# Hybrid attention and DeltaNet step: queries' rotations dealt out in steps, written engine order in two places more

## The chip, the cores and the metric

One NeuronCore of one Trainium2 chip runs the whole step in one launch. The metric is the device time of a launch in microseconds (us). TensorE is called PE, VectorE DVE, ScalarE ACT, GpSimd POOL and SyncE SP.

## The reference

A two-layer decoder trunk works on 1024 prompt tokens and on 8 decode sequences of 4 new tokens, 1056 columns in all. Layer 0 is latent attention (MLA) with a paged cache, layer 1 a gated DeltaNet; each is followed by a SwiGLU feed-forward. The part that the change touches most is the projection of the queries:

```
a = u @ w_in
c_q = rmsnorm(a[..., :Q_LORA], g_q)
c_kv = rmsnorm(a[..., Q_LORA:Q_LORA + KV_LORA], g_kv)
k_r = rope(a[..., Q_LORA + KV_LORA:], pos)
q = (c_q @ w_uq).reshape(b, t, MLA_HEADS, QK_NOPE + QK_ROPE)
q_rope = rope(q[..., QK_NOPE:], pos)
# rope: concat(x1 * cos - x2 * sin, x2 * cos + x1 * sin)
# every layer: x += post_norm(mixer(pre_norm(x))); x += post_norm(ffn(pre_norm(x)))
```

## The kernel before, in words

Activations lie with features on partitions and the 1056 tokens as columns, which are taken in three groups, `GRP`: 384, 384 and 288. A float32 product is made of three matmuls (`mm3`, L261 to L263): each operand is split into a high part, a copy on ACT (L236), and a low part, a subtraction on DVE (L237). `lin` makes one 128-row output block for one group, in one of eight PSUM banks (`ps`) that the elementwise engines have to empty before PE can use it again.

The norms between sublayers are generators, called jobs: squares are summed (`sqs`, `sqr`), PE adds them over partitions with a product by ones (`norm_sum`, L422), DVE takes an inverse square root in ten small operations (`rsqrt`, L291 to L295), PE spreads it over partitions (`norm_spread`, L440), and DVE scales the activations (L344, L353). Each `lin` calls `tick`, which lets the jobs take a step. Outside `with self.order()` a scheduler sets the order of the instructions on each engine from its own priorities; inside it PE, and each engine named, keeps the order in which the code is written.

The query stage in `mla_latents` runs 12 units of three `lin`s, each with a contraction of 3 × 128 rows (`cqh`, `cql`). The first four (`mla_w_uqr`) give the rotary parts of two heads each: ACT copies them out to `qr`, four DMAs issued by POOL write the half-swapped copy (`araw`, L615), DVE then makes `qr*cos`, `araw*sin` and their sum (L620 to L622, 128x1056), ACT and DVE split the result, and POOL issues two DMAs to DRAM (`qrd`). The other eight (`mla_w_uqn`) are the plain parts of the heads, split straight from PSUM into `qh` and `ql` and sent to DRAM (`qd`). The rotary key (`raw[5]`, an `araw` tile as well) is turned after the second plain unit. `absorb` multiplies the decode queries by `w_uk`. The attention that follows loads its queries from `qd` and `qrd` (L1025).

`dn_out` is the output product of the DeltaNet (`out_proj`, L1167), whose norms overlap the beginning of the second feed-forward, `ffn(1)`. `Decode` reads cache pages (`pg`, L1795) beside the output product of layer 0; its two accumulators lie in a pool of that stage.

Of the kernel before, what the change touches and what calls it, by code (L numbers as in the profile page):

```python
# [8 lines left out]
F32 = mybir.dt.float32  # L9
# [6 lines left out]
P = 128  # L16
# [11 lines left out]
LAT = (1, 2)  # L28
NPART = 3
# [6 lines left out]
TICKS = (1, 0), (1, 2), (1, 4), (2, 0), (2, 2), (2, 4)  # L36
# [70 lines left out]
class K:  # L107


    def __init__(self, ctx, tc, I, O):  # L110
# [6 lines left out]
        self.gap = GAP[0]  # L117
# [211 lines left out]
    def boundary_group(self, g, acc, h_src, h_dst, post, pre, u, sq, full):  # L329
# [287 lines left out]
    def rotate(self, raw, sw, cos, sin):  # L617

        nc = self.nc
        nc.vector.tensor_tensor(raw, raw, cos, op=ALU.mult)  # L620
        nc.vector.tensor_tensor(sw, sw, sin, op=ALU.mult)
        nc.vector.tensor_tensor(raw, raw, sw, op=ALU.add)  # L622

    def latent_norm(self, raw, part, out, gn, g):
# [3 lines left out]
        for _ in range(LAT[0]):  # L628
            yield 1
        y = self.norm_sum(sq, g, P * len(part))  # L630
        for _ in range(LAT[1]):
            yield 1
# [17 lines left out]
    def first_layer(self, right, top, h1, h2):  # L650
# [4 lines left out]
        with ExitStack() as left:  # L655
# [11 lines left out]
            OL = top.enter_context(self.scope("mlak", "right")).tile([P, 512], F32, name="OL")  # L667
# [12 lines left out]
            with self.banks(**DBANK):  # L680
                with self.order(*EARLY):


                    side = Decode(self, *smp, OL, tab, msk, wk)
# [7 lines left out]
                    pages(1, 1, 0, 1, False)  # L692
                    self.queue = self.store = nc.gpsimd
                    first = [self.raw_weight(I["mla_w_o"][m]) for m in range(3)]
                    self.queue = nc.sync
                    pages(0, 1, 0, 3)
                    pages(1, 1, 1, 3, False)
                    pages(0, 1, 3, 4)
                    pages(0, 0, 0, 1)
                    pages(1, 1, 3, 4, False)  # L700
                    heads(nc.gpsimd, (0, 0), (0, 1), (1, 0), (1, 1))
                    pages(1, 0, 0, 1, False)
                    pages(0, 0, 1, 4)
                    heads(nc.gpsimd, (2, 0), (2, 1), (3, 0), (3, 1), (4, 0), (4, 1), (5, 0))
# [104 lines left out]
    def mla_project(self, cst):  # L809
# [19 lines left out]
    def mla_latents(self, u, r2, start, ws, araw, gn, wk, cst):  # L829
        nc, I, O, tc, NH = self.nc, self.I, self.O, self.tc, 8  # L830
        with self.banks(ps=8):
# [36 lines left out]


            qs = wk.tile([P, NH * TS_], F32, name="qs")  # L870
            qrs = wk.tile([P, NH * TS_], F32, name="qrs")
            qd = tc.dram_tile([NH, 2, P, TP], F32, name="qd")
            qrd = tc.dram_tile([NH // 2, 2, P, TP], F32, name="qrd")
            qr, sw = {}, {}

            def turned(p):

                self.rotate(qr[p], sw[p], cos, sin)
                for i in range(2):
                    for d in range(2):  # L880
                        nc.gpsimd.tensor_copy(qrs[d * 64:(d + 1) * 64, (2 * p + i) * TS_:(2 * p + i + 1) * TS_],
                                              qr[p][i * 64:(i + 1) * 64, TP:])
                hl = self.S(F32R, "qh"), self.S(F32R, "ql")
                self.split(hl[0][:, :TP], hl[1][:, :TP], qr[p][:, :TP])
                for d in range(2):
                    nc.gpsimd.dma_start(qrd[p, d], hl[d][:, :TP].bitcast(F32))

            def keys():

                sw = araw(0)  # L890
                self.swap(sw, raw[5], nc.gpsimd)
                self.rotate(raw[5], sw, cos, sin)
                h = self.S(F32R, "KRh")
                nc.scalar.activation(h[64:], raw[5][64:], AF.Copy)
                nc.scalar.activation(KR[:64], raw[5][:64], AF.Copy)
                nc.vector.tensor_tensor(KR[64:], raw[5][64:], h[64:].bitcast(F32), op=ALU.subtract)


            pss, absorbed = [], []

            def absorb(hh):
                if not pss:
                    pss.extend(self.psum() for _ in range(2))
                w = absorbed[hh]
                for h4 in range(4):
                    hs = slice((hh * 4 + h4) * TS_, (hh * 4 + h4 + 1) * TS_)
                    for rt in range(2):
                        nc.tensor.matmul(pss[rt][:, hs], w[:, h4 * 256 + rt * P:h4 * 256 + (rt + 1) * P], qs[:, hs],
                                         start=True, stop=True)

            for p in range(NH // 2):
                qr[p], sw[p] = self.S(F32, "qr"), araw(p % 2)
                w = self.weight(I["mla_w_uqr"][p], 384)
                for g in GRP:
                    self.ready(("q", g[0]))
                    ps = self.psum()
                    self.lin(ps, w, cq, 0, g)
                    nc.scalar.activation(qr[p][:, g[0]:g[0] + g[1]], ps[:, :g[1]], AF.Copy)
                self.swap(sw[p], qr[p], nc.gpsimd)
                if p:  # L920
                    turned(p - 1)
            for h in range(NH):
# [12 lines left out]
                if h == 0:  # L935
                    turned(3)
# [1081 lines left out]
```

## Time and profile before

| | |
|---|---|
| three runs | 3140.64, 3153.95, 3154.75 us; median 3153.95 |
| profiled execution | 3136.75 us, its span 3135.1 us |
| mean granted PE clock | 0.982 |
| PE busy | 3022.0 us (96%) |
| DVE busy | 1830.4 us (58%) |
| ACT busy | 1174.2 us (37%) |
| POOL busy | 495.3 us (16%) |

PE is busy nearly throughout, so what can be won is PE's idle time, some 113 us (the span less the busy time), and the time in which its clock was granted at half. A wait is read as "who waited, for what": the engine that stood idle, and the instruction whose end let it go on.

### The profile page before, as it was taken

How to read it: one execution, taken by the hardware profiler on the slowest of the kernel's cores; microseconds unless marked ns; L12 is line 12 of the kernel's file. 1: busy time of each engine (PE TensorE's matmuls, PEld its weight loads, DVE VectorE, ACT ScalarE, POOL GpSimd, SP SyncE). 2: the span in 40 equal slices, each digit the busy share in tenths (PEclk: the TensorE clock that was granted, in tenths of full speed). 3: DMA queues.
4: the chain of work that ended last, by engine and by line, in shares of the span. 5: the costliest groups of instructions: out<-in, count | busy, mean ns of one | idle time of the engine just before them, and what ended most of it. 6: DMA issues, size and time to landing. Idle time of an engine off the chain costs nothing.

```text
span 3135.1 us, 57855 instructions
## 1 busy us (share of the span) xinstructions
PE 3022.0 (96%) x21526; PEld 2800.6 (89%) x21526; DVE 1830.4 (58%) x4234; ACT 1174.2 (37%) x2545; POOL 495.3 (16%) x909
## 2 busy tenths in 40 slices
PE   8799989999999999999999999999989999999998
PEld 8789978888888889999888888888889999999997
DVE  7668757544444444886676667665586444444436
ACT  5345545533333323454444444443542111111121
POOL 1200124344334321121011111111000000000000
PEclk9889999999999999999999999998999999999998
DMA  3564479888788853364322222223231111111113
GB/s 124 165 214 129 134 249 315 291 276 277 241 270 272 270 176 134 122 219 166 124 58 72 79 72 79 74 75 119 82 118 66 41 54 41 44 51 41 48 48 111
DMA packets 286203, 434.52 MB, mean 139 GB/s; under 512 B 60705, under 2 KB 221089, under 8 KB 285922
## 3 DMA queue, kind: packets, MB, share of 16 engines
q1 hardware_dynamic: 220418, 274.51, 27.3%
q0 software_dynamic: 45936, 144.09, 14.2%
q10 hardware_dynamic: 19568, 12.23, 1.3%
q8 instruction: 170, 2.79, 0.4%
q14 instruction: 111, 0.91, 0.1%
HBM read 369.69 MB, written 58.30 MB: 137 GB/s over the span
## 4 chain that ended last, share of the span: by engine, by line
PE 84%; DVE 8%; issue 3%; DMA 3%; ACT 2%; SPq 0%; POOL 0%; ACTq 0%; DVEq 0%; POOLq 0%
PE ps L261 22%; PE ps L262 21%; PE ps L263 21%; PE po L1879 2%; PE sc L1823 2%; PE sc L1100 1%; PE sc L1827 1%; PE tp L1127 1%; PE s L1698 1%; ACT ga L1482 1%; PE s L1695 1%; DVE wl L237 1%; PE ps L422 1%; PE s L1686 1%; PE ga L1605 1%
## 5 line engine op out<-in xcount | busy, mean ns | idle before, releaser
L261 PE MATMUL ps<-oh,wh 128*128 128x384 f32 (+1 forms) x2480 | 816.3, 329 | 6.9 <-ACT wh L236 5.6
L263 PE MATMUL ps<-oh,wl 128*128 128x384 f32 (+1 forms) x2480 | 804.6, 324 | 1.1 <-DVE wl L237 1.1
L262 PE MATMUL ps<-ol,wh 128*128 128x384 f32 (+1 forms) x2480 | 802.6, 324 | 0.0
L236 ACT ACTIVATE wh<-w 128x1024 fp32r<-128x1024 f32 (+3 forms) x300 | 299.2, 1004 | 618.5 <-PE ps L262 523.0
L261 PEld LDWEIGHTS ps<-oh,wh 128*128 128x128 f32 x2480 | 470.0, 190 | 34.1 <-issue 26.0
L263 PEld LDWEIGHTS ps<-oh,wl 128*128 128x128 f32 x2480 | 469.3, 189 | 2.4 <-DVE wl L237 1.9
L262 PEld LDWEIGHTS ps<-ol,wh 128*128 128x128 f32 x2480 | 469.5, 189 | 1.3 <-issue 0.8
L237 DVE TENSOR_TENSOR wl<-w,wh 128x1024 fp32r<-128x1024 f32 (+3 forms) x297 | 342.1, 1159 | 126.8 <-ACT wh L236 124.6
L1795 POOL DMA_DIRECT2D pg<-cache x518 | 283.8, 548 | 460.6 <-PE po L1879 327.3
L261 PE MATMUL ps<-uh,wh 128*128 128x384 f32 (+1 forms) x912 | 310.2, 340 | 8.4 <-ACT wh L236 7.5
L262 PE MATMUL ps<-ul,wh 128*128 128x384 f32 (+1 forms) x912 | 306.1, 336 | 3.0 <-DVE ul L353 3.0
L263 PE MATMUL ps<-uh,wl 128*128 128x384 f32 (+1 forms) x912 | 301.3, 331 | 1.5 <-POOL wl L237 1.5
L261 PE MATMUL ps<-hh,wh 128*128 128x384 f32 (+1 forms) x880 | 294.5, 336 | 0.0
L262 PE MATMUL ps<-hl,wh 128*128 128x384 f32 (+1 forms) x880 | 290.0, 330 | 0.0
L263 PE MATMUL ps<-hh,wl 128*128 128x384 f32 (+1 forms) x880 | 289.3, 329 | 0.0
L261 PEld LDWEIGHTS ps<-uh,wh 128*128 128x128 f32 x912 | 173.6, 190 | 12.2 <-ACT wh L236 7.5
L262 PEld LDWEIGHTS ps<-ul,wh 128*128 128x128 f32 x912 | 173.6, 190 | 5.7 <-DVE ul L353 4.0
L263 PEld LDWEIGHTS ps<-uh,wl 128*128 128x128 f32 x912 | 173.2, 190 | 3.8 <-POOL wl L237 2.0
L261 PEld LDWEIGHTS ps<-hh,wh 128*128 128x128 f32 x880 | 165.3, 188 | 12.1 <-issue 7.9
L262 PEld LDWEIGHTS ps<-hl,wh 128*128 128x128 f32 x880 | 166.2, 189 | 0.9
L263 PEld LDWEIGHTS ps<-hh,wl 128*128 128x128 f32 x880 | 166.0, 189 | 0.1
L568 DVE TENSOR_TENSOR acc<-acc,ps 128x384 f32<-128x384 f32 (+1 forms) x240 | 121.3, 518 | 65.2 <-PE ps L263 63.8
(446 smaller groups left out, 4934.6 us busy)
## 6 DMA issues: line engine op xcount, KB each, us to landing
pg<-cache SPq DMA_DIRECT2D x504, 160.0 KB, 4.0
pg<-cache POOLq DMA_DIRECT2D x510, 128.0 KB, 3.8
w<-ffn_w_in SPq DMA_DIRECT2D x86, 512.0 KB, 4.3
w<-ffn_w_in POOLq DMA_DIRECT2D x52, 512.0 KB, 4.0
w<-ffn_w_out SPq DMA_DIRECT2D x40, 512.0 KB, 4.4
w<-dn_w_in SPq DMA_DIRECT2D x32, 512.0 KB, 3.2
w<-ffn_w_out POOLq DMA_DIRECT2D x26, 512.0 KB, 3.7
qn<-qd SPq DMA_DIRECT2D x64, 128.0 KB, 2.9
```

The lines of the kernel that those rows point to most:

```text
L236: self.nc.scalar.activation(hi, src, AF.Copy)
L237: (lo_eng or self.nc.vector).tensor_tensor(lo, src, hi.bitcast(F32), op=ALU.subtract)
L261: mm(out, ah, bh, start=(i == 0), stop=False)
L262: mm(out, ah, bl, start=False, stop=False)
L263: mm(out, al, bh, start=False, stop=(i == n - 1))
L422: nc.tensor.matmul(ps[:bn, i:i + 1], q[:, b0:b0 + bn], self.ones, start=j == 0, stop=j == len(sq) - 1)
L568: nc.vector.tensor_tensor(acc[m][:, s], acc[m][:, s], po[:, :tn], op=ALU.add)
L1100: mm(o, x["qr"][e][d][:, qsl], KR[:, c], start=False, stop=d == 1)
L1127: self.nc.tensor.transpose(ps[:, j * P:(j + 1) * P], prob[:, kb * P:(kb + 1) * P], self.ident)
L1795: (self.nc.sync, self.nc.gpsimd)[pool].dma_start(self.pages[step, part][c0 + i // 2][:, i % 2], I["cache"][bass.ds(page, 1)].rearrange("o ...
L1823: mm(row(ps, c)[:, :256].rearrange("p (g k) -> p g k", g=2), q(i, c), pgs[c][:, :, i * P:(i + 1) * P], start=i == 0, stop=False)
L1879: nc.tensor.matmul(row(po, c)[:, :256], pT[:, j * P + c * TS_:j * P + (c + 1) * TS_], v, start=j == 0, stop=t < 0 or j == 1)
```

## The change

1. The queries become a function of their own, `mla_queries`, in which PE, ACT and DVE keep the written order. Each rotation is a generator, `away`, and one step of one of them is taken after two of every three `lin`s, from the sixth `lin` on (`WAY`). The key comes first. The product by cos goes from DVE to POOL. Weights are fetched two units ahead. The steps of the latent norms come at ticks (2, 3) in place of (1, 2). `qd` and `qrd` become one DRAM tile for each head and each pair.
2. The three low parts of `mla_w_in` at the start go from POOL to DVE.
3. The two accumulators of `Decode` go to a pool that lives longer, and some issues of pages and head weights change place or queue.
4. In `out_proj` a job waits two more ticks (`LEAD`) before the norm sum of the activations, and `dn_out` with `ffn(1)` keeps PE's written order.
5. The group loop of `dn_start` keeps PE's written order.
6. Each entry of `TICKS`, which sets when the last norm's jobs step in the last chunk of the second feed-forward, is one later.

```diff
-TICKS = (1, 0), (1, 2), (1, 4), (2, 0), (2, 2), (2, 4)
+TICKS = (1, 1), (1, 3), (1, 5), (2, 1), (2, 3), (2, 5)
+LEAD = 2
...
         if post is not None:
+            for _ in range(self.lead):
+                yield 1
             y = self.norm_sum(sq, g, D)
...
-                        ws.append(self.weight(I["mla_w_in"][len(ws)], lo_eng=nc.gpsimd))
+                        ws.append(self.weight(I["mla_w_in"][len(ws)]))
...
+            with self.order(*EARLY[1:3]):
+                return self.mla_queries(raw, cq, ckv, KR, cos, sin, araw, wk, cst)
...
+        def away(x, i, p=None):
+
+            sw = araw(i)
+            self.swap(sw, x, nc.gpsimd)
+            nc.gpsimd.tensor_tensor(x, x, cos, op=ALU.mult)
+            yield 1
+            nc.vector.tensor_tensor(sw, sw, sin, op=ALU.mult)
+            nc.vector.tensor_tensor(x, x, sw, op=ALU.add)
+            yield 1
...
+            hl = [self.S(F32R, "qh")[:, :TP], self.S(F32R, "ql")[:, :TP]]
+            nc.scalar.activation(hl[0], x[:, :TP], AF.Copy)
+            yield 1
+            nc.vector.tensor_tensor(hl[1], x[:, :TP], hl[0].bitcast(F32), op=ALU.subtract)
+            for d in range(2):
+                nc.gpsimd.dma_start(qrd[p][d], hl[d].bitcast(F32))
...
+        go(raw[5], 0)
...
+                if g is GRP[0] and n + 2 < len(units):
+                    ws.append(fetch(units[n + 2]))
+                if lins >= WAY and lins % 3:
+                    step()
+                lins += 1
+            if rotary:
+                go(x, (i + 1) % 3, i)
...
-        self.slack = SLACK[part is not None]
+        self.slack, self.lead = SLACK[part is not None], LEAD
...
-        for g in GRP:
-            self.ready(("u", g[0]))
...
+        with self.order():
+            for g in GRP:
+                self.ready(("u", g[0]))
...
-            with k.weights(*FW[2]):
+            with k.weights(*FW[2]), k.order():
```

On DVE in the query stage, before: rotations of pairs 2 and 3 (`qr`), of which each stands whole in front of the low parts (`ql`) of a plain unit's three PSUM banks; the key (the last row) comes after two plain units.

```order
L237 TENSOR_TENSOR ql_1311<-qr_1151,qh_1310 128x1024
L237 TENSOR_TENSOR ql_1323<-ps_1324,qh_1322 128x384
L237 TENSOR_TENSOR ql_1323<-ps_1336,qh_1322 128x384
L237 TENSOR_TENSOR ql_1323<-ps_1348,qh_1322 128x256
L620 TENSOR_TENSOR qr_1226<-qr_1226,cos_170 128x1056
L621 TENSOR_TENSOR araw_1227<-araw_1227,sin_171 128x1056
L622 TENSOR_TENSOR qr_1226<-qr_1226,araw_1227 128x1056
L237 TENSOR_TENSOR ql_1371<-qr_1226,qh_1370 128x1024
L237 TENSOR_TENSOR ql_1383<-ps_1384,qh_1382 128x384
L237 TENSOR_TENSOR ql_1383<-ps_1396,qh_1382 128x384
L237 TENSOR_TENSOR ql_1383<-ps_1408,qh_1382 128x256
L620 TENSOR_TENSOR araw_595<-araw_595,cos_170 128x1056
```

On DVE at the same place after the change, with the rotations of pairs 2 and 3 again (line numbers are those of the changed kernel; `wl` is the low part of a weight fetched ahead):

```order
L240 TENSOR_TENSOR ql_1437<-ps_1456,qh_1436 128x384
L890 TENSOR_TENSOR araw_1217<-araw_1217,sin_171 128x1056
L891 TENSOR_TENSOR qr_1149<-qr_1149,araw_1217 128x1056
L240 TENSOR_TENSOR ql_1437<-ps_1470,qh_1436 128x256
L240 TENSOR_TENSOR ql_1493<-ps_1494,qh_1492 128x384
L240 TENSOR_TENSOR wl_1509<-w_1506,wh_1508 128x384
L240 TENSOR_TENSOR ql_1493<-ps_1512,qh_1492 128x384
L909 TENSOR_TENSOR ql_1488<-qr_1149,qh_1487 128x1024
L240 TENSOR_TENSOR ql_1493<-ps_1527,qh_1492 128x256
L890 TENSOR_TENSOR araw_1284<-araw_1284,sin_171 128x1056
L891 TENSOR_TENSOR qr_1223<-qr_1223,araw_1284 128x1056
L240 TENSOR_TENSOR ql_1545<-ps_1546,qh_1544 128x384
```

A rotation now stands in two pieces of two and one operations, with one to five emptied banks between them, the cos product is gone from DVE, and the key has come long before.

On POOL, after the change, at the beginning of the queries (L888 is the cos product, L620 the swap's DMAs, `araw_595` the key):

```order
L888 TENSOR_TENSOR araw_595<-araw_595,cos_170 128x1056
L620 DMA araw_1083<-qr_1020 32x1056 x2
L620 DMA araw_1143<-qr_1089 32x1056 x2
L888 TENSOR_TENSOR qr_1020<-qr_1020,cos_170 128x1056
L620 DMA araw_1143<-qr_1089 32x1056 x2
L900 DMA rowsT<-araw_595 64x1056
L620 DMA araw_1217<-qr_1149 32x1056
L888 TENSOR_TENSOR qr_1089<-qr_1089,cos_170 128x1056
```

POOL had only copies and DMA issues there before; now five cos products stand between its DMA issues.

On PE, before, in the beginning of the second feed-forward (`ps<-ones,sqr` is a norm sum over the first group, `ps<-ident,ny` what spreads its root; 29 matmuls stand between the sum and the spread, all but two of them left out here):

```order
L263 MATMUL ps_28475<-oh_27824,wl_27874 128x288
L261 MATMUL ps_28495<-oh_27025,wh_27879 128x288
L422 MATMUL ps_28511<-ones,sqr_28209 128x1 x3
L262 MATMUL ps_28495<-ol_27029,wh_27879 128x288
...
L263 MATMUL ps_28533<-oh_27824,wl_27886 128x288
L440 MATMUL ps_28550<-ident,ny_28513 128x128 x3
L261 MATMUL ps_28559<-oh_27025,wh_27891 128x288
```

On PE, after the change, the same sum and its root's spread:

```order
L266 MATMUL ps_28617<-oh_27710,wl_28597 128x384
L445 MATMUL ps_28687<-ident,ny_28644 128x128 x2
L445 MATMUL ps_28687<-ident,ny_28644 128x32
L427 MATMUL ps_28727<-ones,sqr_28266 128x1 x3
L445 MATMUL ps_28746<-ident,ny_28729 128x128 x3
L264 MATMUL ps_28759<-oh_27014,wh_28604 128x384
```

The spread of the first group's root now stands right behind its sum, with no matmul between them.

## Rows read from the trace of the kernel before

**Rows 1.** Page, part 1: busy time, share of the span and instructions.

```profile
PE 3022.0 (96%) x21526; PEld 2800.6 (89%) x21526; DVE 1830.4 (58%) x4234; ACT 1174.2 (37%) x2545; POOL 495.3 (16%) x909
```

**Rows 2.** What PE waited for, whole span: total us, times, longest.

```profile
PE ps L261 <- DVE ql L237: 16.2, 3, 11.3
...
PE ps L422 <- DVE sqs L405: 9.1, 4, 5.6
...
PE sc L1100 <- DMA Q<-qrd: 4.6, 1, 4.6
...
PE ps L262 <- DVE ul L353: 3.0, 2, 1.9
...
PE s L422 <- DVE sqs L405: 2.6, 1, 2.6
PE sc L1823 <- DMA pg<-cache: 2.6, 3, 1.1
...
PE ps L263 <- POOL wl L237: 1.5, 1, 1.5
```

**Rows 3.** Busy time by stretch: length, engines, then PEclk, DMA share, GB/s.

```profile
92.24:181.55 89.31, 68.98 (x388) 66.89 (x387) 53.13 (x105) 33.49 (x78) 28.06 (x63) 0.85 0.61 210
142.00:157.44 15.44, 4.11 (x26) 3.79 (x24) 5.78 (x7) 3.38 (x7) 3.94 (x8) 0.74 0.69 234
182.00:205.00 23.00, 17.64 (x106) 15.62 (x105) 9.90 (x24) 8.27 (x20) 0.00 (x0) 0.85 0.95 271
```

**Rows 4.** PE in the query stage, in order of time (idle before, releaser).

```profile
129.02 0.34 PE L261 MATMUL ps<-cqh,wh 128*128 128x384 f32 x1
...
129.37 0.34 PE L263 MATMUL ps<-cqh,wl 128*128 128x384 f32 x1
...
134.12 0.61 PE L261 MATMUL ps<-cqh,wh 128*128 128x288 f32 x1 [4.42 <-DVE ql L237]
...
157.44 0.61 PE L261 MATMUL ps<-cqh,wh 128*128 128x288 f32 x1 [11.34 <-DVE ql L237]
```

**Rows 5.** DVE in the query stage, 92.24 to 181.55, by form.

```profile
L621 DVE TENSOR_TENSOR araw<-araw,sin 128x1056 f32<-128x1056 f32 x5 | 6.3, 1251 | 0.0
...
L620 DVE TENSOR_TENSOR qr<-qr,cos 128x1056 f32<-128x1056 f32 x4 | 5.0, 1252 | 0.0
```

**Rows 6.** DVE in the same stage, in order of time.

```profile
150.48 1.26 DVE L620 TENSOR_TENSOR araw<-araw,cos 128x1056 f32<-128x1056 f32 x1 [8.26 <-DMA rowsT<-araw]
...
156.83 4.02 DVE L237 TENSOR_TENSOR ql<-ps,qh 128x384 fp32r<-128x384 f32 x9 [0.23 <-ACT qh L236]
```

**Rows 7.** POOL in the same stage: the end of the key's swap.

```profile
143.05 1.48 POOL L615 DMA_DIRECT2D araw<-araw  x3
```

**Rows 8.** POOL in the first 40 us.

```profile
14.31 2.47 POOL L237 TENSOR_TENSOR wl<-w,wh 128x1024 fp32r<-128x1024 f32 x1 [0.72 <-ACT wh L236]
```

**Rows 9.** DVE in the same stretch.

```profile
10.81 0.54 DVE L405 TENSOR_TENSOR sqr<-sqr,sq 128x384 f32<-128x384 f32 x1
...
14.46 2.73 DVE L405 TENSOR_TENSOR sqr<-sqr,sq 128x384 f32<-128x384 f32 x1
```

**Rows 10.** PE where the second feed-forward begins.

```profile
2319.43 1.44 PE L422 MATMUL ps<-ones,sqs 128*128 128x1 f32 x6 [5.63 <-DVE sqs L405]
...
2332.47 0.72 PE L422 MATMUL ps<-ones,sqr 128*128 128x1 f32 x6
...
2339.04 0.51 PE L440 MATMUL ps<-ident,ny 128*128 128x128 f32 x3 [1.92 <-DVE ny L295]
```

**Rows 11.** DVE ahead of the sum at 2319.43, and the root behind it.

```profile
2296.10 1.15 DVE L344 SCALAR_TENSOR_TENSOR acc<-acc,nw,r 128x384 f32<-128x384 f32 x2 [1.16 <-ACT r L432]
...
2316.83 2.54 DVE L405 TENSOR_TENSOR sqs<-sqs,sq 128x384 f32<-128x384 f32 x4
2320.91 0.16 DVE L423 TENSOR_SCALAR nx<-ps 128x3 f32<-128x3 f32 x1 [1.53 <-PE ps L422]
...
2322.88 0.16 DVE L295 SCALAR_TENSOR_TENSOR ny<-nt,ny 128x3 f32<-128x3 f32 x1
```

More of the change, by code (lines that the diff above doesn't have):

```diff
@@ L28 @@
 LAT = (1, 2)
+LATE = (2, 3)
+WAY = 5
 NPART = 3
@@ L615, in swap @@
             eng.dma_start(sw[a:a + 32], raw[b:b + 32])
[L617 to L622, printed above, removed]
     def latent_norm(self, raw, part, out, gn, g):
@@ L627, in latent_norm @@
         sq = self.latent_squares([raw[m][:, s] for m in part], g)
-        for _ in range(LAT[0]):
+        for _ in range(self.late_norm[0]):
             yield 1
         y = self.norm_sum(sq, g, P * len(part))
-        for _ in range(LAT[1]):
+        for _ in range(self.late_norm[1]):
             yield 1
@@ L666, in first_layer @@
             self.ua = right.enter_context(self.scope("ua", "right"))
-            OL = top.enter_context(self.scope("mlak", "right")).tile([P, 512], F32, name="OL")
+            keep = top.enter_context(self.scope("mlak", "right"))
+            OL = keep.tile([P, 512], F32, name="OL")
+            accs = [keep.tile([P, 256], F32, name=self.nm("dacc")) for _ in range(2)]
             self.aa = top.enter_context(self.scope("aa", "right"))
@@ L692, in first_layer @@
                     pages(1, 1, 0, 1, False)
+                    pages(1, 0, 0, 1, False)
                     self.queue = self.store = nc.gpsimd
@@ L888, in keys @@
[L888 to L909, printed above, removed]
@@ L947, in mla_latents @@
                     absorb(0)
-            for t0, _ in GRP:
-                self.ready(("kv", t0))
-            for k in range(2):
-                nc.gpsimd.dma_start(O["rowsT"][k * P:(k + 1) * P], raw[3 + k])
-            nc.gpsimd.dma_start(O["rowsT"][2 * P:], raw[5][:64])
-            new = cst.tile([P, 3 * TS_], F32, name="new")
-            for k in range(3):
-                nc.scalar.activation(new[:, k * TS_:(k + 1) * TS_], raw[3 + k][:, TP:], AF.Copy)
-            cn = cst.tile([TS_, 256], F32, name="cn")
@@ L971, in mla_latents @@
-            return (qd, qrd, first), (ckv, KR), (QS, new, cn)
+        for t0, _ in GRP:
+            self.ready(("kv", t0))
+        for k in range(2):
+            nc.gpsimd.dma_start(O["rowsT"][k * P:(k + 1) * P], raw[3 + k])
+        new = cst.tile([P, 3 * TS_], F32, name="new")
+        while len(ways) > 1:
+            step()
+        for k in range(3):
+            nc.scalar.activation(new[:, k * TS_:(k + 1) * TS_], raw[3 + k][:, TP:], AF.Copy)
+        cn = cst.tile([TS_, 256], F32, name="cn")
@@ new lines, in mla_queries @@
+        ps = self.psum()
+        for k in range(2):
+            nc.tensor.transpose(ps[:TS_, k * P:(k + 1) * P], new[:, k * TS_:(k + 1) * TS_], self.ident)
+        nc.scalar.activation(cn, ps[:TS_, :256], AF.Copy)
+        QS = cst.tile([P, 1024], F32, name="QS")
+        nc.gpsimd.memset(QS[64:, 512:768], 0.0)
+        nc.gpsimd.memset(QS[:64, 768:], 0.0)
+        absorb(1)
+        while ways:
+            step()
+        for i, src in enumerate((pss[0][:, :256], pss[1][:, :256], qrs[:64], qrs[64:])):
+            o = QS[(0, 0, 0, 64)[i]:(P, P, 64, P)[i], i * 256:(i + 1) * 256]
+            nc.scalar.activation(o.rearrange("p (b h s) -> p b h s", b=DB, s=DS),
+                                 src.rearrange("p (h b s) -> p b h s", b=DB, s=DS), AF.Copy)
@@ L973, in mla_attend @@
+        self.late_norm = LAT
+        return (qd, qrd, first), (ckv, KR), (QS, new, cn)
     def mla_attend(self, SC, q, kv, cst):
@@ L1769, in __init__ @@
         self.turning, self.valued = [], []
-        self.accs = [wk.tile([P, 256], F32, name=k.nm("dacc")) for _ in range(2)]
         for step in self.coming[0][:2]:
```

158 lines of the change are left out of this document (81 added, 77 removed).

## The prediction

> **What bounds the kernel now.** I read the busy shares first: PE is busy 3022.0 us, 96% [rows 1], of a span of 3135.1 us. No other engine is near; what can be won is PE's 113 us of idle time and what its clock loses. The list of PE's waits [rows 2] shows where they are: 16.2 us in three waits for the low part `ql` of the queries, 9.1 us in four for sums of squares (`sqs`), 4.6 us once for queries coming from DRAM, and smaller ones. Then the busy time by stretch [rows 3]: the query stage takes 89.31 us, in which PE is busy 68.98 and idle 20.3, at a mean granted clock of 0.85. In order of time [rows 4] two waits stand out there, 4.42 us ending at 134.12 and 11.34 us ending at 157.44. DVE's rows tell why the longer one is so long: DVE itself stands idle 8.26 us for a DMA, the key's half-swap, and then turns the key before it empties nine PSUM banks' worth of `ql` [rows 6]. The last three DMAs of that swap went out at 143.05 on POOL [rows 7], three microseconds before PE stopped (157.44 − 11.34 = 146.1).
>
> So it is an order problem: DVE reaches the key's rotation before the swapped key is there, and everything that would free a bank is queued behind it.
>
> **The queries.** What would the stage take without waits? Matmuls with 384 columns follow each other every (129.37 − 129.02)/2 = 0.175 us at full speed [rows 4]. The stage has 12 units of two groups of 384 columns and one of 288, nine matmuls each: 12 × 9 × (0.175 + 0.175 + 0.131) = 52.0 us (0.131 is 0.175 scaled by 288/384, an estimate). Of the 89.3 us, 20.3 are idle; the other 17 are the half-clock stretches and small matmuls (norm sums, the absorption). The mean clock of 0.85 bounds the half-speed loss at 0.15 × 89.3 = 13.4 us, so the small matmuls take at least 17 − 13.4 = 3.6; I take 5, and a floor of 57 us. Around the long wait the clock is 0.74 [rows 3]: the engine had stood idle, and it came back at half clock. If the waits go, part of this goes too.
>
> What the change does here: the key is turned first and its swap is issued before any query unit, and every other rotation is used some eight to twelve `lin`s after its swap was issued, 8 × 1.4 = 12 us or more, against (150.48 − 143.05) = 7.4 us from the issue of a swap's last DMAs to the DVE instruction that waited for it [rows 6, 7]. So the 8.26 us are covered by PE's own work, and both long waits, 15.8 us, should go. DVE's work: 53.13 us in the stage now [rows 3]. The five cos products, 5 × 1.25 = 6.3 us [rows 5, 6], leave it: 46.9 us. In their place POOL works, and here the trace speaks against the change. POOL's subtraction of 128x1024 took 2.47 us [rows 8], and scaled to 1056 columns a cos product is estimated at 2.55. While it ran, DVE's addition with both inputs in SBUF took 2.73 us in place of 0.54 [rows 9]: it ended only after POOL. If every cos product holds DVE for its whole length, DVE loses 5 × 2.55 = 12.7 us, and has 59.6 us to fill, a little over PE's floor of 57. Low parts taken from PSUM have one input there and should be able to run meanwhile, which is some of what stands between rotations in the new order. I take 65 to 73 us for the stage, 69 in the middle: **−20 us**. Bounds: if both the 15.8 us and all of the 13.4 us went, and nothing came, −29; if only the 8.26 us of waiting for the key went, −8.
>
> The 4.6 us wait for queries from DRAM comes after the stage, in a stretch where the DMA engines are busy 0.95 of the time and the clock is 0.85 [rows 3]. Its loads are issued by SP behind others that depend on the stage's last results, so I let it stay: 0, with −7 (the wait and about as much of the half clock, 0.15 × 23 = 3.4) if the separate DRAM tiles let loads go early.
>
> **The start.** Low parts on POOL cost PE 1.5 us directly, and 3.0 us through `ul`, which DVE couldn't finish under POOL's subtraction [rows 2, 8, 9]: 4.5 us. On DVE the three cost 3 × 1.25 = 3.7 us by the rows of 128x1056 [rows 5], and stand in front of `ul` as well. Between 0 and −4: −2.
>
> **The second feed-forward.** The sum at 2319.43 waits 5.63 us for `sqs`; the root of the next sum is waited for 1.92 us, although PE had other matmuls between 2332.47 and 2339.04 [rows 10]. DVE works without a pause from 2296.10 to 2319.4 [rows 11], so two more ticks don't bring `sqs` earlier: they push DVE's first group's work back, and PE's sum comes two `lin`s later (about 4 us), so that the wait stays about where it was. In the new order the first group's root is wanted right behind its sum, with no matmul between. The chain costs at least 2320.91 to 2323.04, 2.1 us, on an unoccupied DVE [rows 11], and up to the 6.6 us from 2332.47 to 2339.04 on an occupied one [rows 10]; so 2.5 to 6 in place of 1.92. Against that stands up to 5.6 if the two ticks do cover the first wait. **+2**, between −4 and +6.
>
> **The rest.** The pages are waited for 2.6 us [rows 2]; two SP issues fewer lie ahead of them: −1, between −3 and 0. The accumulators' move costs no instruction. `dn_start`: 2.6 us for `sqs` [rows 2] go when the sum stands where it is written, but small products now stand directly behind the gate's matmuls and wait for DVE: 0, ±3. The last chunk's ticks can move only what remains of the 9.1 us beyond the 5.6 [rows 2], 3.5 us in three waits of which not all are there: −1, between −2 and +1.
>
> **Sum.** −20 − 2 + 2 − 1 + 0 − 1 = −22 us on the profiled execution's 3136.75, which gives 3115. That execution is 17.2 us below the median of the three runs, 3153.95, and near the fastest of them, 3140.64; the runs lie in two clumps. On the median the same sum gives 3132. I give 3130.
>
> **The rivals.**
> *DVE and POOL become the bound of the query stage (22%).* If the cos products hold DVE for all of their length and the banks of a unit wait for a rotation in each of the nine units concerned, the 59.6 us of DVE work stretch by the waits for ACT which a written order doesn't let DVE step around. Against it: half of the new DVE rows read PSUM. For it: DVE 2.73 for 0.54 [rows 8, 9]. The stage then takes 77 to 82 us, the gain is 10, the total −12 + 2 for the rest: 3144 by the median, no change that can be told. The page "SBUF — State Buffer" of the Trainium skill, section "Who interferes with whom", says the same in general: an operation of VectorE with two SBUF inputs and one of GpSimd that reads SBUF exclude each other for the whole of the one that started first. The trace agrees: 0.54 became 2.73 under a POOL subtraction of 2.47 [rows 8, 9].
>
> *The written order makes it slower (8%).* DVE stops at a product by sin until the swap has landed, and in a written order nothing behind it moves. If POOL, with five cos products of 2.55 us between its DMA issues, is so late that each of the five rotations holds DVE for 10 us (the key's wait was 8.26 [rows 6]), DVE sets the stage: 59.6 + 50 = 110 us, +20, and with −2 for the rest the total is +18: 3172. It decides from 9.5 us a rotation on ((89.3 + 15.7 + 2 − 59.6)/5); at 6 us each the stage is as long as now. Against it: 7.4 us from issue to use are all that the key's swap needed [rows 6, 7], and swaps are issued eight `lin`s, some 12 us, ahead.
>
> *More than is forecast (12%).* The wait for queries from DRAM goes too, −7, and the clock stays full in the stage, −26 there: −35 in all, 3119 by the median.
>
> **How the numbers follow.** The forecast itself has 58%: −16 to −30, 3124 to 3138 by the median, and lower by up to 17 if the runs fall like the profiled one. What this measurement can tell from no change is about 0.5%, 15.7 us. The forecast's sum passes that by 6 us only, so I count nine tenths of its 58% and the 12% as faster: 64%. The same: the rest of it, all of the first rival: 28%. Slower: 8%. The range for 8 in 10 reaches from 3106, the high gain seen on the lower clump of the runs, to 3150, which takes in most of the first rival and leaves out the slower one.
>
> **What would show it.** In the new trace the two waits for `ql` (4.42, 11.34) are gone; DVE never waits over 2 us for a swap; the stretch from the first `cqh` matmul to the last of the absorption takes 65 to 73 us at a clock over 0.92; additions and products by sin that run beside a cos product take up to 2.7 us; the wait for `Q` of 4.6 us is still there; the root behind `ones,sqr` in the second feed-forward is waited for 2.5 us or more. It is wrong if PE waits for `ql` or for evictions in many short pieces in the queries (first rival), if DVE waits for the swaps (second), or if runs of before and after differ by their clump rather than by this stage.

## The result, and the profile after

The changed kernel takes 3163.38 us (median of ten runs, 3159.47 to 3171.09), the kernel before 3153.36 in ten runs beside it (3140.64 to 3158.56): a ratio of 1.0040, 95% interval 1.0025 to 1.0055. It is 10 us slower; 24 us less had been forecast, and the time lies outside the range.

The trace shown before is one of the quickest executions of its kernel. A second trace of the same kernel (base, below) is 15.9 us longer, nearly all of it in the DeltaNet heads, which the change doesn't touch. So the traces are compared by stage; between before and base, which are one program, a stage other than the heads differs by 0.1 to 2.3 us, against which its change after is to be held. Each length is from the first or last matmul of a kind to the next in a trace's order of time:

| stage, up to | before | base | after | after − before |
|---|---|---|---|---|
| start, first `cqh` | 92.2 | 92.8 | 88.2 | −4.0 |
| queries, last of the absorption | 89.3 | 87.9 | 82.6 | −6.7 |
| attention, last `po<-pt,vl` | 240.5 | 242.2 | 250.5 | +10.0 |
| pages, first `hh` of layer 0 | 179.0 | 177.4 | 183.8 | +4.8 |
| decode and feed-forward, first `uv` | 603.0 | 602.6 | 596.8 | −6.2 |
| to the last gate matmul | 355.0 | 357.3 | 360.1 | +5.1 |
| DeltaNet heads | 693.1 | 708.2 | 703.5 | +10.4 |
| to the first `hh` of the second feed-forward | 143.2 | 142.8 | 148.4 | +5.2 |
| its chunks | 670.5 | 670.5 | 672.1 | +1.6 |
| to the end | 69.3 | 69.5 | 72.8 | +3.5 |
| span | 3135.1 | 3151.0 | 3158.8 | +23.7 |

Without the heads the change costs 13.3 us by these traces (12.4 against base), near the 10 us of the medians. The busy shares of the page (as in [rows 1]) are nearly the same:

```profile
PE 3027.7 (96%) x21526; PEld 2806.5 (89%) x21526; DVE 1836.9 (58%) x4232; ACT 1169.4 (37%) x2543; POOL 502.7 (16%) x913
```

What PE waited for over the whole span, to be held against [rows 2]:

```profile
PE ps L427 <- DVE sqs L410: 17.9, 5, 5.7
PE ps L264 <- ACT wh L239: 15.4, 5, 7.9
PE ps L445 <- DVE ny L298: 12.5, 6, 4.9
PE sc L1129 <- DMA Q<-qrd: 10.4, 3, 7.1
...
PE ps L264 <- DVE acc L1196: 4.7, 1, 4.7
...
PE sc L1852 <- DMA pg<-cache: 4.1, 2, 2.6
PE bp L1345 <- DVE baT L1341: 3.5, 2, 2.9
```

The 16.2 us for `ql` are gone, as forecast. In their place stand 6.2 us more for `sqs` (17.9 for 9.1 and 2.6), 5.8 more for `Q<-qrd`, 4.7 for `acc` (0.7 before) and 3.5 for `baT` (none before).

**In the query stage** these are PE's two long waits, in order of time, and the one at the scores behind it:

```profile
107.51 1.44 PE L427 MATMUL ps<-ones,sqs 128*128 128x1 f32 x6 [4.79 <-DVE sqs L410]
...
125.17 1.21 PE L427 MATMUL ps<-ones,sqs 128*128 128x1 f32 x6 [5.62 <-DVE sqs L410]
...
198.96 0.45 PE L1129 MATMUL sc<-KR,Q 128*128 128x128 f32 x1 [7.07 <-DMA Q<-qrd]
```

DVE ahead of the first of them, in the root behind it, and ahead of the second:

```profile
101.87 0.56 DVE L240 TENSOR_TENSOR kvl<-araw,kvh 128x384 fp32r<-128x384 f32 x1 [0.59 <-ACT kvh L239]
102.35 1.25 DVE L890 TENSOR_TENSOR araw<-araw,sin 128x1056 f32<-128x1056 f32 x1
103.70 3.28 DVE L891 TENSOR_TENSOR araw<-araw,araw 128x1056 f32<-128x1056 f32 x1
106.90 0.55 DVE L410 TENSOR_TENSOR sqs<-sqs,sq 128x384 f32<-128x384 f32 x1
...
110.16 2.65 DVE L297 SCALAR_TENSOR_TENSOR nt<-nt,nx 128x3 f32<-128x3 f32 x1
...
122.71 2.41 DVE L410 TENSOR_TENSOR sqs<-sqs,sq 128x288 f32<-128x288 f32 x1 [1.35 <-ACT sq L406]
```

POOL beside them:

```profile
103.41 2.45 POOL L888 TENSOR_TENSOR qr<-qr,cos 128x1056 f32<-128x1056 f32 x1
...
110.32 2.46 POOL L888 TENSOR_TENSOR qr<-qr,cos 128x1056 f32<-128x1056 f32 x1
...
122.39 2.41 POOL L888 TENSOR_TENSOR qr<-qr,cos 128x1056 f32<-128x1056 f32 x1
```

The addition of squares that PE's first sum wants stands behind the previous group's low part and behind the key's rotation, whose last addition takes 3.28 us instead of 1.26, as a cos product runs on POOL. Before the second sum DVE first waits 1.35 us for ACT's squares, and then the addition of squares is itself stretched by a cos product, to 2.41 us (0.45 in cos_dve, where POOL makes none). So POOL's products hold up each of the two sums by some 2 us. Even an operation on three columns took 2.65 us instead of 0.16 beside one of them. The stage's busy time, and two stretches behind it (columns as in [rows 3]):

```profile
88.25:170.89 82.64, 67.05 (x388) 64.78 (x387) 58.97 (x101) 33.33 (x80) 40.98 (x68) 0.89 0.65 218
175.00:185.00 10.00, 8.71 (x63) 8.07 (x62) 6.88 (x12) 5.22 (x9) 0.00 (x0) 1.00 0.86 236
185.00:195.00 10.00, 3.42 (x14) 3.01 (x14) 1.83 (x9) 1.02 (x4) 0.00 (x0) 0.61 1.04 270
```

DVE is busy 58.97 us where 59.6 had been worked out, but not full: 71% of 82.64. PE is idle for 15.6 us (20.3 before): 10.4 for `sqs`, 2.9 for weights' high parts (`wh`) and 2.2 for a copy of new latents (`new`).

**The first pair's loads**, SP's queue in order of time:

```profile
175.65 0.33 SPq L246 DMA_DIRECT2D w<-mla_w_uk  x1
...
177.50 1.16 SPq L1054 DMA_DIRECT2D Q<-qrd  x2
...
181.27 3.71 SPq L1054 DMA_DIRECT2D Q<-qrd  x6
185.03 8.42 SPq L1054 DMA_DIRECT2D qn<-qd  x12
193.54 1.09 SPq L1054 DMA_DIRECT2D Q<-qrd  x2
```

The end of the same queue in the trace before:

```profile
185.93 8.40 SPq L1025 DMA_DIRECT2D qn<-qd  x12
194.57 1.09 SPq L1025 DMA_DIRECT2D Q<-qrd  x2
```

PE was through with the queries 10.7 us earlier than before (170.89, not 181.55), but the last two of these loads, the ones awaited for 7.07 us, go out behind twelve others and only 1.0 us earlier than before.

**Behind the decode steps** the first matmul waited 5.59 us for `wh` before (the first row), and waits 1.48 now:

```profile
1167.47 0.69 PE L261 MATMUL ps<-oh,wh 128*128 128x384 f32 x1 [5.59 <-ACT wh L236]
```

```profile
1167.49 0.44 PE L264 MATMUL ps<-oh,wh 128*128 128x384 f32 x1 [1.48 <-ACT wh L239]
...
1535.44 1.46 PE L1345 MATMUL bp<-tab,baT 128*128 128x16 f32 x6 [2.86 <-DVE baT L1341]
...
2336.17 1.44 PE L427 MATMUL ps<-ones,sqs 128*128 128x1 f32 x6 [5.74 <-DVE sqs L410]
...
2354.29 0.41 PE L264 MATMUL ps<-oh,wh 128*128 128x384 f32 x1 [4.73 <-DVE acc L1196]
...
2371.03 0.90 PE L445 MATMUL ps<-ident,ny 128*128 128x128 f32 x3 [4.77 <-DVE ny L298]
```

The other rows are of later stages. The wait of the gates' small product in `dn_start` (2.86) is new. In the second feed-forward the first sum waits as before (5.74; 5.63 in [rows 10]); a wait for DVE to empty a bank has grown (4.73; 0.67 before), and so has that for the root, now directly behind its sum (4.77 for 1.92).

### The profile page after: what moved, and what is told of

Its sections match the earlier page's. It is cut to its first block, busy times and chain, and to the rows that moved or that the text cites. A ratio compares the mean times of both kernels' runs of the same rounds, so it can differ in the third digit from the quotient of the medians.

```text
span 3158.8 us, 57866 instructions
## 1 busy us (share of the span) xinstructions
PE 3027.7 (96%) x21526; PEld 2806.5 (89%) x21526; DVE 1836.9 (58%) x4232; ACT 1169.4 (37%) x2543; POOL 502.7 (16%) x913
## 4 chain that ended last, share of the span: by engine, by line
PE 84%; DVE 8%; DMA 3%; ACT 2%; issue 2%; SPq 0%; POOL 0%; DVEq 0%; ACTq 0%
PE ps L264 22%; PE ps L265 21%; PE ps L266 21%; PE po L1908 2%; PE sc L1852 2%; PE sc L1856 1%; PE sc L1129 1%; PE tp L1156 1%; DVE wl L240 1%; PE s L1728 1%; ACT ga L1512 1%; PE s L1725 1%; PE ga L1635 1%; PE s L1716 1%; PE ps L427 1%
## 5 line engine op out<-in xcount | busy, mean ns | idle before, releaser
L264 PE MATMUL ps<-uh,wh 128*128 128x384 f32 (+1 forms) x912 | 310.6, 341 | 11.2 <-ACT wh L239 11.0
L264 PEld LDWEIGHTS ps<-uh,wh 128*128 128x128 f32 x912 | 175.5, 192 | 13.8 <-ACT wh L239 11.2
```

Source lines behind the costliest of these rows:

```text
L264: mm(out, ah, bh, start=(i == 0), stop=False)
```

## The experiments

All ratios are to the kernel before on the same chip, beside the run; its median was between 3143.6 and 3153.4 us from one such comparison to the next, and the changed kernel was timed in the first alone. So ratios are held against each other within one comparison, and all else is read from the stages of single traces, as in the table above.

**base**: the kernel before, unchanged.

> The kernel before once more, unchanged, for a second trace: ten runs of it lie in two groups, two or three near 3141 and the rest at 3152 to 3158, and the trace shown is of the faster group. Theory A (the 10 us that the changed kernel lost among the DeltaNet heads, 1560 to 2170 us, belong to such a group and not to the change): a trace of the slower group shows the same heads 8 to 12 us longer with more half-clock stretches there. Rival B (the change did it): the heads take the same 609 us in this trace as well, whichever group it is.

3152.68 us, span 3151.0. Heads 708.2 us, not 693.1. Two stretches of 88 and 79 us in the heads, first in the trace shown before, then in base:

```profile
1712.00:1800.00 88.00, 86.84 (x631) 76.80 (x629) 56.38 (x159) 39.68 (x112) 14.30 (x22) 1.00 0.25 72
2191.00:2270.00 79.00, 73.09 (x527) 63.58 (x527) 39.85 (x133) 39.26 (x113) 1.90 (x1) 0.98 0.25 77
```

```profile
1712.00:1800.00 88.00, 84.36 (x582) 74.70 (x580) 58.33 (x153) 36.39 (x107) 13.96 (x22) 0.94 0.25 71
2191.00:2270.00 79.00, 70.92 (x456) 60.55 (x455) 34.97 (x120) 32.41 (x101) 2.75 (x2) 0.81 0.24 74
```

PE does less in the same stretch at a lower granted clock. The stretches are the same by time, not quite by the work: base falls behind from 2 to 9 us in the first, and from 8 to 16 us in the second up to the end of the heads, which is where nearly all of the difference arises. Theory A, though the heads are 15 us longer and not 8 to 12. Over all traces of this study the heads took 693 to 710 us, with no order by kernel. What the changed kernel lost there need not be the change's.

**q_only**: the kernel before with the new query function alone (a cut of the edit).

```diff
+            with self.order(*EARLY[1:3]):
+                return self.mla_queries(raw, cq, ckv, KR, cos, sin, araw, wk, cst)
```

> The kernel before with the first part of the change alone: the new query function, nothing else. Theory A (the queries gain some 7 us on PE, which the wait for queries from DRAM behind them gives back): the stretch from the first cqh matmul to the last of the absorption takes 82 to 84 us instead of 89.3, the waits for Q<-qrd add up to 9 to 11 us instead of 4.6, and the first probabilities are transposed within 2 us of the time before (203.3); the whole is within 5 us of before, all 10 us of the slower median come from the other parts. Rival B (the query part itself makes the kernel slower): the first transposes come more than 3 us late, or the whole is 8 to 12 us slower than before.

1.0074 (1.0046 to 1.0101). Queries 83.4 us, attention 248.0, first transposes at 204.80, 1.5 us later than before; the waits for `Q<-qrd` are 9.7 us: up to there theory A holds. But from attention's end to the first `hh` it takes 194.0 us, not 179.0, with pages in their old order. By the whole time rival B is right.

**uk_pool**: later pairs' `w_uk` and `w_uv` on POOL's queue.

```diff
+        self.queue = nc.gpsimd if p else nc.sync
-        wu, wv = (self.weight(I[n][p], 512) for n in ("mla_w_uk", "mla_w_uv")) if p else first
+        wu, wv = [self.weight(I[n][p], 512) for n in ("mla_w_uk", "mla_w_uv")] if p else first
+        self.queue = nc.sync
```

> The changed kernel, the raw w_uk and w_uv of the later head pairs loaded by POOL's queue instead of SP's, so that the loads of the first pair's queries stand right behind what SP has issued for the query stage. Theory A (SP's queue order sets the start of the scores: four weight loads of later pairs, one of them waiting for a split on DVE until 175.6, stand ahead of the first pair's loads): the first load of qn or Q goes out before 172 instead of 177.5, the waits for Q<-qrd fall from 10.4 us to under 5, and the first transposes come 5 to 8 us earlier than 201.9; the time falls by 5 to 8 us against the changed kernel. Rival B (the DMA engines, or the last writes of qd at 168.9, are the limit): the loads go out earlier but land no earlier, the wait stays 8 to 11 us, the time stays within 2 us of the changed kernel.

1.0070 (1.0049 to 1.0091). The first load goes out at 166.13, 11 us earlier than after, as theory A has it; but the last two go out at 190.24 (193.54), PE waits 8.6 us for them, and the first transposes come at 199.77, 2.1 us earlier; attention takes 248.3 us for 250.5. In front_kept, with the same edit, the last two went out at 193.01. The weights ahead in the queue were worth 2 us at most; rival B is nearer, but see q_early.

**cos_dve**: the cos products on DVE.

```diff
-            nc.gpsimd.tensor_tensor(x, x, cos, op=ALU.mult)
+            nc.vector.tensor_tensor(x, x, cos, op=ALU.mult)
```

> The changed kernel with the cos products back on DVE, at the same places. Theory A (POOL's cos products hold DVE, five times about 2.2 us more than the operations need, and the two waits of PE for sqs, 4.8 and 5.6 us, contain part of it): DVE operations between 93 and 131 show no stretched ones, DVE gains 11 us of stalls and spends 6.3 on the products, the two waits for sqs fall from 10.4 to 6 to 8 us in sum and the stage is 2 to 4 us shorter. Rival B (DVE is the scarcer engine, POOL the better place): the waits grow to 12 us or more, the stage is 2 to 5 us longer. By either the end differs by less than that, since the loads of the queries set the start of the scores.

1.0098 (1.0071 to 1.0125). Queries 91.8 us, 9 us more. The key's addition takes 1.26 us again, but PE waits in the stage as follows:

```profile
PE ps L427 <- DVE sqs L410: 16.9, 3, 7.4
PE ps L264 <- ACT wh L239: 3.8, 1, 3.8
```

Rival B, though 9 us and not 2 to 5. The row ahead of the longest of these waits tells why:

```profile
132.98 1.26 DVE L888 TENSOR_TENSOR qr<-qr,cos 128x1056 f32<-128x1056 f32 x1 [4.77 <-DMA araw<-qr]
```

The product overwrites the tile that the swap's DMAs read, so DVE, in its written order, stands still until they are through, 12.2 us in three such waits, with the squares' addition behind it. At this place POOL is the cheaper engine for it; cos on DVE at a later place, behind the swap, was not tried.

**front_kept** and **front_late**: the last three parts taken back (on top of uk_pool); in front_late the sums three ticks later as well.

```diff
-TICKS = (1, 1), (1, 3), (1, 5), (2, 1), (2, 3), (2, 5)
+TICKS = (1, 0), (1, 2), (1, 4), (2, 0), (2, 2), (2, 4)
-LEAD = 2
+LEAD = 0
-        with self.order():
-            for g in GRP:
+        for g in GRP:
-            with k.weights(*FW[2]), k.order():
+            with k.weights(*FW[2]):
...
-LATE = (2, 3)
+LATE = (5, 3)
```

> The changed kernel with the loads of later pairs' w_uk and w_uv on POOL's queue and with the last three parts of the change taken back (written order and lead in the second feed-forward, written order in the DeltaNet's first loop, ticks). Theory A (the losses behind 1500 us, some 14 us without the heads, belong to these three parts): first transposes at 199 to 201 as with the queue moved, 4 us lost again at the pages, 6 us won at the end of the decode steps, and from there on the differences to before stay within 2 us up to the end, but for the heads, where the clock of the single execution decides: 3130 to 3133 us if the heads run as in the faster group, 3146 to 3149 if as in the slower one. Rival B (something in front makes the later stages slower as well): the difference grows by more than 4 us behind the last head.

> The kernel of front_kept with the latent norms' sums three ticks later (LATE 5, 3 instead of 2, 3). Theory A (in the query stage PE waits for sqs, 4.8 and 5.6 us, because its written order puts the sum where DVE, in its own written order, still has the rotation and the kv low parts before the squares' addition): the two waits go to under 1.5 us in sum and the query stage is 6 to 10 us shorter than the 82.6 of the changed kernel; the scores' start gains nothing like it if the loads are still behind. Rival B (DVE is full, the waits only move): PE waits elsewhere, for evictions or ql, and the stage is within 3 us of 82.6.

front_kept: 0.9988 (0.9971 to 1.0005). To the gates 354.7 us, to the first `hh` 142.5, chunks 670.5, end 69.4: all as before, theory A; the pages took 186.0, 7 us more than before where 4 had been expected. front_late: 1.0028 (1.0009 to 1.0047). Its query stage takes 81.2 us. The waits moved, rival B:

```profile
PE ps L445 <- DVE ny L298: 12.0, 2, 6.3
PE ps L986 <- ACT new L982: 2.2, 1, 2.2
PE ps L427 <- DVE sqs L410: 1.9, 2, 1.5
```

Its last two loads go out at 185.65, and the first transposes come at 195.46, 6.0 us earlier than in front_kept; but the pages took 198.9 us, not 186.0, more than attention had won.

**order_only** (LEAD 0, old ticks) and **lead_only** (no written order in the second feed-forward).

> The changed kernel with LEAD 0 and the ticks of before: of the last three parts in the second feed-forward the written order alone. Theory A (it is the written order that costs): from the DeltaNet's last small product to the first hh matmul 4 to 6 us more than before (143.2), 1.6 us more in the chunks that follow, and the end as before (0 to 1). Rival B (the lead costs): 0 to 2 us more up to the first hh matmul.

> The changed kernel without the written order in the second feed-forward; lead and the new ticks stay. Theory A (it is the written order that costs): the beginning of the second feed-forward within 2 us of before, no growth in the chunks, and at the end 2 to 3.5 us more, from the ticks. Rival B (the lead costs there): 4 to 6 us more up to the first hh matmul. Rival C (the order, not the ticks, costs at the end): the end within 1 us of before.

1.0014 (0.9995 to 1.0032) and 1.0018 (1.0000 to 1.0036). To the first `hh`: 142.7 with the order alone, 145.1 with the lead alone, 148.4 with both. Neither theory: it takes both to lose 5 us. Each brings one of the two waits, the order that for the root (3.83 us), the lead that for `acc` (3.87). The chunks take 672.0 with the order and 670.5 without, and the end 71.8 and 69.0: there rival C is right, the order costs, and the ticks by themselves cost nothing.

**q_early**: the fourth rotary load ahead of the twelve.

```diff
             rotary(e, d)
+        if not p:
+            rotary(1, 1)
         for pr in range(1, 4):
             plain(pr)
...
-            if kb == 6:
+            if kb == 6 and p:
                 rotary(1, 1)
```

> The changed kernel, in which the first pair's fourth rotary part is loaded ahead of the plain parts of its later queries instead of behind them. It is the one PE waited 7.1 us for: SP issued it at 193.5, behind twelve loads that took 8.4 us to issue and are needed later. Theory A (the place of this one load on SP sets the start of the scores): the wait of 7.1 us falls under 2, the first transposes come 5 to 7 us earlier than 201.9, and attention ends 4 to 6 us earlier than 421.4. Rival B (the DMA engines are full, share 0.95 to 1.05 from 185 to 195, and it does not matter which load goes first): the waits at the scores only move, the first transposes come within 2 us of 201.9.

1.0031 (1.0018 to 1.0045). SP's queue, and PE's waits at the scores:

```profile
181.17 5.43 SPq L1054 DMA_DIRECT2D Q<-qrd  x8
186.65 12.57 SPq L1054 DMA_DIRECT2D qn<-qd  x16
```

```profile
PE sc L1131 <- DMA Q<-qrd: 5.7, 3, 2.1
```

The 7.07 us are 1.67, the first transposes come at 197.10 (201.88) and attention ends at 416.38 (421.37). Theory A: this wait was the place of one load in SP's order. It is about half of what was lost there: from the end of the queries to the first transposes it still takes 26.6 us (31.0 in after, 21.8 before), with two more waits of 2 us each for `Q<-qrd`. This edit together with that of uk_pool was not run.

**front_q**: q_early with the last three parts taken back.

> The kernel of q_early with the last three parts of the change taken back. Theory A: as q_early up to the decode steps, and no loss behind 1500 us: the sum of the stages outside the heads is 6 to 10 us under before; 0 to 5 us of it may be lost at the pages of the cache, whose loads start where attention ends. Rival B (what attention gains the pages take back, as in front_late, where 12 us went between the end of attention and the first page scores): the difference to before at the first hh matmul is +2 us or more although attention ended 5 us or more earlier.

3133.98 us to 3143.62 of before: **0.9971 (0.9956 to 0.9985)**, faster than both kernels. On the same chip q_early took 3152.99: the last three parts cost 19 us there by the medians, and 14.5 by the four stages of the traces that they touch (359.2, 150.4, 672.1, 72.3 in q_early; 356.4, 143.2, 670.5, 69.4 in front_q). Outside the heads the sum is 5.5 us under before, a little less than theory A's 6 to 10, with 4.1 us lost at the pages.

**accs_lo** and **accs_lo_q**: the kernel before with the accumulators and the three low parts moved; the second with the early load.

> The kernel before with two small parts of the change alone: the accumulators in the longer-lived pool, and the three low parts at the start on DVE. Theory A (the accumulators' move is what ends the wait of 5.2 to 5.6 us for wh behind the decode steps; the low parts' move is worth 4 us): first cqh at 88 to 88.7, the wait at 1161 falls under 2 us, and the end is 8 to 10 us earlier than before in the same group of runs: ratio 0.997. Rival B (the gain behind the decode steps came from the new order of pages and heads, not from the accumulators): the wait stays over 4 us; 4 us faster in all.

> The kernel of accs_lo with the early load of q_early. Theory A (the 4.6 us wait for Q<-qrd of the kernel before is the same load behind the same twelve): the wait falls under 1.5 us, attention ends 3 to 5 us earlier still, and the whole is 10 to 14 us faster than before: ratio 0.996. Rival B (the pages take it back): the same up to the end of attention, then within 2 us of accs_lo.

1.0035 (1.0021 to 1.0048) and 1.0027 (1.0012 to 1.0042). Start 87.5 and 88.1; the stage that ends with the decode steps 599.2 and 598.1, and its wait for `wh`:

```profile
1175.40 0.69 PE L261 MATMUL ps<-oh,wh 128*128 128x384 f32 x1 [1.48 <-ACT wh L236]
```

Every trace with the accumulators moved has 596.8 to 599.5 there and a wait of 1.48, the three without 602.2 to 603.0 and 5.2 to 5.7. Both gains of accs_lo's theory A are there, but the pages took 195.8 and 192.8 us, not 179.0, and the whole is slower, not 8 to 10 us faster. For accs_lo_q neither theory holds: the wait for `Q` fell to 0.3 us, but PE then waited 6.9 for `wh` from 191.75 on, and attention ended no earlier (421.04; 417.28 in accs_lo).

**q_pe, q_peact, q_free** (front_q with the written order in the queries on PE alone, on PE and ACT, on none) and **old_pages** (front_q with the old order of pages). The edit of q_free's query stage:

```diff
-            with self.order(*EARLY[1:3]):
+            with nullcontext():
                 return self.mla_queries(raw, cq, ckv, KR, cos, sin, araw, wk, cst)
```

> The kernel of front_q with the query stage in written order on PE alone; DVE and ACT as the scheduler sets them. Theory A (DVE's written order makes PE wait for sqs: an addition of squares stands behind the kv low parts and the rotation although its squares are done): the waits for sqs fall from 10.4 us to under 4 and the stage from 81.7 to 72 to 77 us. Rival B (the amount and the dependences of DVE's work, not its order): the waits for sqs, ny and ql add up to 8 to 14 us as before, and the stage is within 3 us of 81.7 or longer.

> The kernel of front_q with the query stage in written order on PE and ACT, DVE as the scheduler sets it. Theory A: as q_pe, within 2 us. Rival C (ACT's written order makes the squares late, not DVE's): as front_q, 80 to 83 us, while q_pe is at least 4 us shorter.

> The kernel of front_q with no written order in the query stage at all. Theory A (the written order of PE is needed too, as it puts the sums where they are): sums come where the scheduler thinks them ready, the waits for sqs vanish, and waits for ql return in part, 3 to 8 us; the stage is 73 to 80 us. Rival B: the stage is 84 us or more, nearly that of before (89.3), and it is the written order that won what was won.

> The kernel of front_q with the order of pages and head weights of before; the accumulators stay in the longer-lived pool. Theory A (the new order is made for the earlier end of attention: with the old one pages are issued late): the way from the end of attention to the first hh matmul of layer 0, 179.0 us before and 183.1 in front_q, becomes 190 to 196 us, as in accs_lo (195.8) and q_only (194.0). Rival B (in those two it was something else, as the memory that the accumulators leave): within 3 us of 183.1 or better.

Ratios 0.9983 (0.9965 to 1.0000), 0.9974 (0.9956 to 0.9992), 0.9963 (0.9946 to 0.9980); queries 80.6, 80.4 and 80.1 us, front_q 81.7. Rival B of q_pe: the order in which DVE does it isn't the point; q_peact is as q_pe, its theory A. In q_free PE waits in the stage as it did before the change, in smaller pieces:

```profile
PE ps L264 <- DVE ql L240: 10.5, 3, 5.6
PE ps L445 <- DVE ny L298: 1.8, 1, 1.8
```

The waits for `sqs` vanished, as its theory A has it, but `ql` costs 10.5 us and not 3 to 8, and 80.1 us are at the edge of its 73 to 80. Rival B is refuted: what won 6 to 9 us against before and base is the rest of the new function (key first, rotations spread, cos on POOL, weights two units ahead, later norm steps, split DRAM tiles), not the written order. What each of these is worth was not measured. old_pages: 1.0024 (1.0004 to 1.0044), with 197.6 us at the pages for 183.1: theory A by its number, the new page order is worth 14.5 us beside the new queries.

## Why the prediction was wrong, point by point

**The queries, −20: mis-sized, −6.7.** Right: both waits for `ql` went, DVE never waited for a swap, DVE's work came to 58.97 us (59.6), and operations beside cos products were stretched. PE's floor of 57 was right too: 82.64 less 15.6 us idle and at most 9.1 of half clock (0.11 × 82.64) leaves 58. The step that failed is "both long waits, 15.8 us, should go", and with it "I take 65 to 73 us for the stage": the two waits went, but 10.4 us of waits for `sqs` came in their place, so that PE's idle time fell by 4.7 us and not by 15.8. The step set DVE's work as one sum beside PE's floor and asked only whether it fits. The clock rose to 0.89, not over 0.92. My reading, not shown apart: DVE's work isn't a sum but chains of squares, sum on PE, root, spread and scale, three times over, each link in line behind rotations. What the runs show is that PE meets it as waits for `sqs` (10.4), `ny` (12.0 in front_late) or `ql` (10.5 in q_free), while the stage stays at 80 to 83 us. The rival "DVE and POOL become the bound" gave 77 to 82 us and came nearest in time, but not by its mechanism: DVE is busy for 71% of the stage, and PE does not wait for evictions in many short pieces. Which link of the chains is the longest was not measured.

**The scores, 0, with −7 if loads go early: the wait grew, 4.6 to 10.4 us.** The step that its loads "are issued by SP behind others that depend on the stage's last results, so I let it stay: 0" let the wait stay as long as it was. What stayed is the moment at which the last loads go out, 194.57 before, 193.54 after, behind twelve others in SP's queue; so what was won in the queries turned into waiting and half clock (0.61 from 185 to 195). Attention ended only 0.7 us earlier than before. q_early shows it for the longest wait, by moving one load; front_late, whose last loads go out 8 us earlier, agrees.

**The accumulators, "costs no instruction": −3 to −6, missed.** The move cut a wait of 5.59 us for `wh` behind the decode steps to 1.48. I had priced the edit by its instructions and not by what waits for the memory. That it is the pool's release which the weight waited for was argued from the wait, not shown apart; nor was the move run without the three low parts, which lie 1100 us ahead of that wait.

**The pages, −1: +4.8** (2.64 + 1.44 us of waits for pages; the granted clock is 0.75 from 426 to 440, 0.87 from 427 to 440 before). The step took the wait for pages, 2.6 us, to fall with two issues fewer ahead; it grew. Why the old order loses 14 to 19 us in all four kernels that change something ahead of it (q_only, accs_lo, accs_lo_q, old_pages), and the new one 2 to 7, but 20 in front_late, stays open; that pages, weights and `oT` loads fall differently on two queues each time is a guess.

**`dn_start`, 0 ± 3: +5.1**, though single traces vary here: six with the written order took 359.0 to 360.1 us, twelve without it 354.5 to 358.3, so the means are 3.3 us apart. The doubt named in the step, small products behind the gates' matmuls, shows in the rows: 2.86 and 0.68 us of waits for `baT`.

**The second feed-forward, +2: +5.2**, inside the bounds. The root behind its sum waited 4.77 us (2.5 to 6 forecast) and the first wait stayed (5.74 for 5.63). What was missed is that lead and order cost it only together, and 1.6 us of written order in the chunks. **The end, −1: +3.5**, of which the order alone makes 2.5; I had not priced it there at all. The ticks alone cost nothing; order, lead and ticks together ended in 72.2 to 72.8 us in four traces, 71.8 with the order alone.

**The start, −2: −4.0**, the full size of the waits.

**The base of the sum.** The heads differ by 15.1 us between two traces of one kernel. I had seen two clumps of runs, and chose the forecast by them without a stage to put them in. Two slips of the prediction's arithmetic change nothing: eight `lin`s of 1.4 us are 11.2 us and not 12, and in the first rival −10 with −2 for the rest makes 3142, not 3144.

## What to carry to other kernels

Before crediting a stage with its saved time, look for the next thing that the stage's end waits for and ask what sets that moment: here it was when a DMA queue came to its last loads, and nearly the whole gain of the queries disappeared in it, half of it by the position of one load. A written order is worth what its author knows of the other engines: two of three here put a small product or a root's spread directly behind its producer, where the scheduler had left matmuls between, and cost 3 and, together with the lead, 5 us. When two traces of one kernel differ by 16 us, compare by stage and leave out the stage that varies on its own.

## What the hardware showed unexpectedly

Each of the five cos products on POOL (2.41 to 2.47 us) held one DVE operation, and cost DVE much the same whatever the size of that operation: 2.0 us on 1056 columns (3.28 for 1.26) and on 288 (2.41 for 0.45), 2.3 to 2.6 on three (2.42, 2.65 and 2.75 for 0.16). So a long POOL operation also stops a chain of small ones, such as the root's ten. The page "SBUF — State Buffer" of the Trainium skill, section "Who interferes with whom", says that the one that comes second waits for the whole of the other and names no smallest size. The trace agrees as to the length; but two of the five DVE operations begin, by their rows, 0.16 and 0.27 us ahead of the POOL product and are held all the same, which stays open. And the heads of the same kernel took 693.1 or 708.2 us, with a granted clock of 0.98 or 0.81 in a stretch of 79 us, though the program is the same.
